# A two-sequence encoder trunk on one core: other costs on the emission clock, a scatter operand laid out by token, and attention weights as products of rounded halves

## The chip, the core and the metric

The kernel runs on one core of a Trainium2 chip as one program. The metric is the device time of one execution in microseconds (us). Three executions of the kernel before took 3652.63, 3653.04 and 3654.71 us (median 3653.04). Engines are named as in the profile: PE (TensorE; PEld is its weight load), DVE (VectorE), ACT (ScalarE), POOL (GpSimd) and SP, which here only issues transfers.

## The reference

Two sequences of 256 tokens and 1024 features go through the same two layers with the same weights.

```python
def trunk(x, p, ...):
    for i in range(DEPTH):                       # DEPTH = 2
        if i % N_MIXERS == 0:
            h = dilated_mixture_attention(x, attn_w_qkv[j], attn_w_out[j])   # layer 0
        else:
            h = short_conv_mixer(x, conv_w_in[j], conv_kernel[j], conv_w_out[j])   # layer 1
        x = layer_norm(DEEPNORM_ALPHA * x + h, ln1_gain[i], ln1_bias[i])
        f = peer_channel_mixer(x, peer_w_query[i], peer_sub_keys[i], peer_u[i], peer_v[i])
        x = layer_norm(DEEPNORM_ALPHA * x + f, ln2_gain[i], ln2_bias[i])
        x = x + jax.nn.sigmoid(x @ ple_w_gate[i]) * (p[i] @ ple_w_proj[i])
```

`dilated_mixture_attention` multiplies x (256x1024) by a matrix of 1024x9216, attends in three groups of 8 heads, and multiplies by a 1024x1024 output matrix. `peer_channel_mixer` scores each token against sub-keys, takes for each of 8 heads the 16 best of 16384 experts, and adds `gelu(x . u[e]) * gate * v[e]` over the 128 chosen experts; u and v have 16384 rows of 1024 numbers. All of it is in float32.

## The kernel before, in words

**Two threads.** `thread_a` carries the first sequence and `thread_b` the second. Each is a generator that emits instructions and yields a cost; the main loop always continues the thread with the smaller sum of costs. Thread B begins at `T0B`, thread A at 0. The sum of costs is the emission clock. It also sets the priorities by which a scheduler, at build time, writes one fixed order for each engine. On the chip each engine works through its own order. `GCOST` is the cost of four gathers, `RCOST` of one eighth of a routing, and 11, 2.5 and 22 (lines 223 to 305) those of attention.

**Experts, two ways.** Thread A gathers: for each of its two blocks of 128 tokens and each of 128 chosen experts it fetches a row of u per token (line 472, POOL issues, 128 rows of 4 KB), DVE multiplies it with x and sums (line 489), and later the same with v (line 510): 512 gathers in a layer into a ring of 8 buffers. Thread B computes densely: it reads the whole of u and v in blocks of 128 experts (`dense_u`, `down`), so 256 blocks of 512 KB in a layer, and multiplies the hidden values by a gate matrix G that is zero where an expert was not chosen. `scatter` builds G for 16 blocks at a time: DVE writes one-hot rows (line 583, tile I1) and their product with the gates, in two float16 halves (line 585, tile I0, the moving operand); PE multiplies them, one matmul for each token (line 599, 32 columns; line 592, 16 columns, for the first 16 blocks); ACT and DVE move the result out (lines 600, 601). In I0 the token is the innermost index, so the 32 columns of one token lie 64 bytes apart. While B routes, `hold` keeps A from emitting gathers.

**Attention.** `token_major_steps` (line 111) multiplies x with `w_qkv` and `w_out`: a block of 512 KB holds two slices of 128x512, and four float32 matmuls read it. There are 80 such blocks, or 320 products, in each thread's attention. `wload` brings a block into the ring `raw` (8 buffers), which also holds the norm parameters and the routing's weights while the first pools are open (`open1`). `attend` computes scores, a softmax (lines 250 to 257) and the values (line 272).

**Routing** (`route`) is a long chain of small DVE instructions (top-16 searches, lines 349 to 357, and index arithmetic to line 420). `finish` is the last gated product of a layer (`ple`).

Of the kernel before, what the change touches and what calls it, by code (L numbers as in the profile page):

```python
# [8 lines left out]
F32 = mybir.dt.float32  # L9
F8 = mybir.dt.float8e4  # L10
F16 = mybir.dt.float16
# [35 lines left out]
def encoder_trunk(ctx: ExitStack, tc: tile.TileContext, A: dict):  # L47
# [37 lines left out]
    iota16 = T(cp, [P, CH, 2 * TG], "iota16", F16)  # L85
# [10 lines left out]
    def wload(e, src, n=WB):  # L96
        raw = e.raw()[:, :n]
        nc.sync.dma_start(raw, src)
# [5 lines left out]
    def wblocks(e, name, nb, cols=512):  # L104
        kpb = WB // cols
        src = A[name]
        for b in range(src.shape[1]):
            w = wload(e, src[nb, b])
            yield b * kpb, kpb, w.rearrange("p (c n) -> p c n", n=cols)

    def token_major_steps(e, xt, name, nb, ps, kcs=KC):
        ps += [e.mm() for _ in range(NT)]
        for c0, n, w in wblocks(e, name, nb):
            for t in range(NT):
                for c in range(n):
                    kc = c0 + c
                    mm(ps[t], xt[:, kc, t * P:(t + 1) * P], w[:, c], kc == 0, kc == kcs - 1)
            yield 2.5
# [70 lines left out]
    def attention(e, g, x):  # L189
        ap = e.attn  # L190
        xt = e.xt()
        first = e.mask is None
        for kb in range(0, KC, 2):
            nc.scalar.dma_start(xt[:, kb:kb + 2].rearrange("p c s -> p (c s)"), A[f"xT{g}"][:, kb * S:(kb + 2) * S])
# [5 lines left out]
        ot = e.xt()  # L200
        done = {}

        def project(hp):
            base = (hp // 2) * 9 + (0 if hp % 2 == 0 else 5)
            qkT = T(ap, [P, NG, 4, S], "qkT", bufs=2)
            for gr in range(NG):
# [16 lines left out]
                yield 11  # L223
# [4 lines left out]
            yield 11  # L228
            if hp % 2 == 0:
                v2 = T(ap, [P, NT, 4, HD], "v2", bufs=2)  # L230
                ps = token_major(e, xt, "w_qkv", base + 4)
                for t in range(NT):
                    nc.scalar.activation(v2[:, t].rearrange("p a d -> p (a d)"), ps[t], AF.Copy)
                yield 11
            else:
                v2 = done[hp - 1][2]
            done[hp] = qkT, v01, v2

        def attend(hp):
# [20 lines left out]
            def values(hh, t, pr):  # L260
# [11 lines left out]
                nc.scalar.activation(ot[:, h, sl], ov[:, :P], AF.Copy)  # L272

            held = []
            for hh in range(2):
                for t in range(NT):
# [3 lines left out]
                    yield 2.5  # L280
# [24 lines left out]
        yield 22  # L305
# [236 lines left out]
    def peer_dense(e, i, xt, sel, spill, newx, pre):  # L542
# [30 lines left out]
        def scatter(c):  # L573
# [3 lines left out]
            for tg in range(S // TG):  # L577
                ts = slice(tg * TG, (tg + 1) * TG)
                if tg % 2 == 0:
                    t2 = slice(tg * TG, (tg + 2) * TG)  # L580
                    I1 = T(dp, [P, CH, 2 * TG], "I1", F16, bufs=1)
                    I0w = T(dp, [P, 2 * CH * 2 * TG], "I0", F16, bufs=2).rearrange("p (q a b) -> p q a b", q=2, a=CH)
# [3 lines left out]
                I0 = I0w[:, :, :, (tg % 2) * TG:(tg % 2 + 1) * TG]  # L586
                ps = T(e.phid, [P, 512], "hid").rearrange("p (a q b) -> p a q b", q=2, b=CH)
                gv = G[:, :, ts]
                if c < SCU:
                    for k in range(TG):  # L590
                        for q in range(2):
                            nc.tensor.matmul(ps[:, k, 0], J[:, tg * TG + k], I0[:, q, :, k], start=q == 0, stop=q == 1)
# [5 lines left out]
                for k in range(TG):  # L598
                    nc.tensor.matmul(ps[:, k], J[:, tg * TG + k], I0[:, :, :, k], start=True, stop=True)  # L599
# [81 lines left out]
    R1 = 8  # L681
# [14 lines left out]
    def open1():  # L696
# [4 lines left out]
        xp = p1.enter_context(tc.tile_pool(name="xt1", bufs=2))  # L701
# [3 lines left out]
        e.xt = ring(xp, [P, KC, S], "x")  # L705
# [30 lines left out]
    GCOST = 6.0  # L736
    T0B = 280.0
    RCOST = 21.0
# [96 lines left out]
def _layout(inputs):  # L835
# [46 lines left out]
    put("iota16", np.repeat(np.arange(CH, dtype=np.float16), 2 * TG)[None])  # L882
# [36 lines left out]
```

## Time and profile before

| | us |
|---|---|
| median of three runs | 3653.04 |
| profiled execution | 3650.72 |
| its span | 3648.9 |
| PE busy in the span | 3337.4 |
| DVE busy | 2191.9 |
| ACT busy | 559.7 |
| POOL busy | 1399.5 |

The profile is of one execution; the span is the time between its first and its last instruction. It was cut into ten stages by the first instructions of the norms (line 160), of the gate matrix (line 568) and of thread B's last sums (line 631): A's attention to 331.4 us, B's attention beside A's routing and first gathers to 741.7, B's routing to 917.7, the first gate matrix to 959, layer 0's dense part to 1892, `finish` and convolution of both threads with A's routing to 2330, B's routing to 2505, the gate matrix to 2545, layer 1's dense part to 3500, and the end.

### The profile page before, as it was taken

The numbers are of one execution on the slowest core, as the hardware profiler recorded it, in microseconds if no ns is written. First come the engines' busy times: TensorE is split into PE (matmuls) and PEld (weight loads), VectorE is DVE, ScalarE is ACT, GpSimd is POOL, SyncE is SP. The second block draws the span as 40 slices with busy tenths as digits, with TensorE's granted clock in tenths as the row PEclk, the third lists the DMA queues.
The fourth block names the chain that finished last, engine by engine and source line by source line (L and its number), as shares of the span: only waits on it lengthen the run. The fifth ranks groups of instructions, "written<-read, shape, count | busy, mean of one in ns | idle before, by whom it ended". The sixth has DMA issues, their size and how long they took to land. (4 is left out here: it accounts for less than half of the span.)

```text
span 3648.9 us, 42774 instructions
## 1 busy us (share of the span) xinstructions
PE 3337.4 (91%) x15472; PEld 2224.3 (61%) x15472; DVE 2191.9 (60%) x4766; ACT 559.7 (15%) x1380; POOL 1399.5 (38%) x1476
## 2 busy tenths in 40 slices
PE   9998999987699999999999859894999999999937
PEld 4555565566466666666667538583576666666623
DVE  0002796047976677766651284488866767676683
ACT  1222223223110001000011112132000001000001
POOL 0110574000355555555630040001655555555560
PEclk9999999999799999999999979896999999999978
DMA  6434797343599999999985564442999999999993
GB/s 210 136 119 127 280 347 262 110 141 116 192 377 368 374 374 368 376 374 372 391 312 169 157 222 156 141 140 75 390 366 360 369 368 360 370 375 375 406 401 113
DMA packets 280436, 1007.19 MB, mean 276 GB/s; under 512 B 31648, under 2 KB 33056, under 8 KB 280224
## 3 DMA queue, kind: packets, MB, share of 16 engines
q0 software_dynamic: 147456, 536.94, 38.7%
q1 hardware_dynamic: 124128, 448.85, 34.7%
q10 hardware_dynamic: 8640, 18.68, 1.5%
q8 instruction: 122, 2.00, 0.2%
q14 instruction: 90, 0.74, 0.1%
HBM read 999.09 MB, written 5.24 MB: 275 GB/s over the span
## 5 line engine op out<-in xcount | busy, mean ns | idle before, releaser
L472 POOL DMA_INDIRECT g<-in_u_dram,ei x512 | 635.1, 1241 | 572.8 <-DVE g L489 219.9
L102 PE MATMUL out<-ur,hs 128*128 128x512 f32 x1824 | 819.8, 600 | 35.8 <-ACT k L649 30.0
L102 PE MATMUL hid<-bx1T,ur 128*128 128x256 f32 x3584 | 817.9, 382 | 4.5 <-DVE G L601 4.5
L472 POOL DMA_INDIRECT g<-in_v_dram,ei x512 | 628.9, 1228 | 424.1 <-DVE acc L510 158.5
L102 PEld LDWEIGHTS hid<-bx1T,ur 128*128 128x128 f32 x3584 | 677.6, 191 | 137.7 <-issue 47.1
L510 DVE SCALAR_TENSOR_TENSOR acc<-g,cf,acc 128x1024 f32<-128x1024 f32 x508 | 652.1, 1284 | 56.0 <-DMA g<-in_v_dram,ei 46.4
L489 DVE SCALAR_TENSOR_TENSOR g<-g,xa 128x1024 f32<-128x1024 f32 x512 | 608.8, 1225 | 49.6 <-DMA g<-in_u_dram,ei 49.5
L102 PEld LDWEIGHTS out<-ur,hs 128*128 128x128 f32 x1824 | 339.2, 192 | 411.4 <-issue 371.1
L102 PE MATMUL mm<-raw,x 128*128 128x512 f32 x1280 | 569.9, 596 | 10.3 <-DMA x<-in_xT_dram 8.2
L102 PEld LDWEIGHTS mm<-raw,x 128*128 128x128 f32 x1280 | 237.4, 192 | 274.4 <-issue 269.2
L250 DVE SCALAR_TENSOR_TENSOR k<-tr,mask 128x512 f32<-128x512 f32 x32 | 22.0, 688 | 404.0 <-PE tr L247 404.0
L599 PEld LDWEIGHTS <-J 128*128 128x128 fp8e4 x3584 | 223.0, 112 | 62.1 <-issue 37.2
L599 PE MATMUL hid<-I,J 128*128 128x32 f16 x3584 | 245.1, 232 | 8.7 <-ACT hs L554 5.1
L102 PE MATMUL out<-bx1T,ur 128*128 128x256 f32 x1024 | 232.9, 389 | 16.9 <-ACT k L369 10.8
L102 PEld LDWEIGHTS out<-bx1T,ur 128*128 128x128 f32 x1024 | 198.5, 195 | 47.3 <-ACT k L369 13.2
L400 POOL TENSOR_TENSOR ci<-sif 128x32 f32<-128x32 f32 x64 | 17.4, 292 | 535.2 <-ACT sif L386 534.6
L600 ACT ACTIVATE G<-hid 128x256 f32<-128x256 f32 x224 | 85.9, 384 | 876.5 <-PE hid L599 876.5
L102 PE MATMUL out<-ur,x 128*128 128x512 f32 x448 | 200.6, 603 | 12.6 <-DVE x L555 12.6
L601 DVE TENSOR_TENSOR G<-G,hid 128x256 f32<-128x256 f32 x224 | 92.7, 417 | 195.2 <-ACT G L600 195.2
L214 POOL TENSOR_TENSOR rm<-k,rope 128x128 f32<-128x128 f32 x48 | 27.2, 566 | 433.4 <-ACT k L210 433.2
L555 DVE SCALAR_TENSOR_TENSOR hs<-hs,G 128x512 f32<-128x512 f32 x112 | 77.2, 689 | 178.3 <-ACT hs L554 178.3
L554 ACT ACTIVATE hs<-hid 128x512 f32<-128x512 f32 x112 | 66.9, 597 | 717.5 <-PE hid L102 484.5
(182 smaller groups left out, 2651.1 us busy)
## 6 DMA issues: line engine op xcount, KB each, us to landing
ur<-in_uT_dram SPq DMA_DIRECT2D x256, 512.0 KB, 6.9
ur<-in_v_dram SPq DMA_DIRECT2D x256, 512.0 KB, 6.7
raw<-in_w_qkv_dram SPq DMA_DIRECT2D x144, 512.0 KB, 4.3
raw<-in_w_q_dram SPq DMA_DIRECT2D x32, 512.0 KB, 4.2
ur<-in_w_q_dram SPq DMA_DIRECT2D x32, 512.0 KB, 3.6
raw<-in_c_in_dram SPq DMA_DIRECT2D x24, 512.0 KB, 3.8
ur<-in_c_in_dram SPq DMA_DIRECT2D x24, 512.0 KB, 3.6
raw<-in_w_out_dram SPq DMA_DIRECT2D x16, 512.0 KB, 4.4
```

Source lines behind the costliest of these rows:

```text
L102: nc.tensor.matmul(out, a, b, start=first, stop=last)
L214: nc.gpsimd.tensor_tensor(m1, st[:, :, :2 * RH], c, op=ALU.mult)
L250: nc.vector.scalar_tensor_tensor(prf, sc, SCALE, mask[:, t], op0=ALU.mult, op1=ALU.add)
L400: eng.tensor_tensor(dst[:, :, off:off + n], src[:, :, 1, 0:n], src[:, :, 0, a0:a0 + 1].to_broadcast([P, 2, n]), op=ALU.add)
L472: nc.gpsimd.indirect_dma_start(out=t, out_offset=None, in_=tab, in_offset=bass.IndirectOffsetOnAxis(ap=idx, axis=0))
L489: nc.vector.scalar_tensor_tensor(r, r, 1.0, x[t], op0=ALU.mult, op1=ALU.mult, accum_out=dots[:, k:k + 1])
L510: nc.vector.scalar_tensor_tensor(acc[t], r, c, acc[t], op0=ALU.mult, op1=ALU.add)
L554: nc.scalar.activation(hs, hid, AF.Gelu)
L555: nc.vector.scalar_tensor_tensor(hs, hs, 1.0 / GSC, G[:, 2 * pr:2 * pr + 2], op0=ALU.mult, op1=ALU.mult)
L599: nc.tensor.matmul(ps[:, k], J[:, tg * TG + k], I0[:, :, :, k], start=True, stop=True)
L600: nc.scalar.activation(gv, ps[:, :, 0].rearrange("p a b -> p b a"), AF.Copy)
L601: nc.vector.tensor_tensor(gv, gv, ps[:, :, 1].rearrange("p a b -> p b a"), op=ALU.add)
```

## The change

Three things are changed. First, the two matrices of attention: each block is split by ACT into a copy rounded to float32r (`hi`) and by DVE into the rounded rest (`lo`), x and the attention's output likewise, and each product becomes three matmuls, hi hi, hi lo and lo hi. The ring `raw` shrinks from 8 to 3 buffers; rings of 3 and 2 hold `hi` and `lo`. Second, in `scatter` the token becomes the outer index of I1 and I0, so the 32 columns of one token lie side by side. Third, five costs and the start of thread B on the emission clock.

```diff
+    def split(hi, lo, src):
+        nc.scalar.activation(hi, src, AF.Copy)
+        nc.vector.tensor_tensor(lo, src, hi.bitcast(F32), op=ALU.subtract)
...
+        hi, lo = e.hi()[:, :n], e.lo()[:, :n]
         nc.sync.dma_start(raw, src)
-        return raw
+        split(hi, lo, raw)
+        return hi, lo
...
     def mm(out, a, b, first, last):
-        nc.tensor.matmul(out, a, b, start=first, stop=last)
+        if not isinstance(a, tuple):
+            nc.tensor.matmul(out, a, b, start=first, stop=last)
+            return
+        nc.tensor.matmul(out, a[0], b[0], start=first, stop=False)
+        nc.tensor.matmul(out, a[0], b[1], start=False, stop=False)
+        nc.tensor.matmul(out, a[1], b[0], start=False, stop=last)
...
-                nc.scalar.activation(ot[:, h, sl], ov[:, :P], AF.Copy)
+                split(ot[0][:, h, sl], ot[1][:, h, sl], ov[:, :P])
...
-                    nc.vector.tensor_tensor(I1, iota16, ic[:, t2].unsqueeze(1).to_broadcast([P, CH, 2 * TG]), op=ALU.is_equal)
-                    bc = [P, 2, CH, 2 * TG]
-                    last = nc.vector.tensor_tensor(I0w, I1.unsqueeze(1).to_broadcast(bc), gT[:, :, t2].unsqueeze(2).to_broadcast(bc), op=ALU.mult)
+                    nc.vector.tensor_tensor(I1, iota16, ic[:, t2].unsqueeze(2).to_broadcast([P, 2 * TG, CH]), op=ALU.is_equal)
+                    bc = [P, 2 * TG, 2, CH]
+                    last = nc.vector.tensor_tensor(I0w, I1.unsqueeze(2).to_broadcast(bc), gT[:, :, t2].rearrange("p q b -> p b q").unsqueeze(3).to_broadcast(bc), op=ALU.mult)
...
-                    nc.tensor.matmul(ps[:, k], J[:, tg * TG + k], I0[:, :, :, k], start=True, stop=True)
+                    nc.tensor.matmul(ps[:, k].rearrange("p q b -> p (q b)"), J[:, tg * TG + k], I0[:, k].rearrange("p q a -> p (q a)"), start=True, stop=True)
...
-    R1 = 8
+    R1 = 3
+    H1 = 3
+    L1 = 2
...
-    GCOST = 6.0
-    T0B = 280.0
-    RCOST = 21.0
+    GCOST = 5.2
+    T0B = 420.0
+    RCOST = 14.0
+    PCOST = 17.0
```

The new costs move instructions on every engine. On DVE, in B's attention after A's routing, the order before holds only the softmax (mask and scale, maximum, reciprocal; the gathers have been stopped by then):

```order
L250 SCALAR_TENSOR_TENSOR k_749_3065<-tr_3061,mask_105 128x512
L252 TENSOR_REDUCE nm_3067<-k_749_3065 128x1
L256 RECIPROCAL rd_3071<-den_3069 128x1
L250 SCALAR_TENSOR_TENSOR k_776_3158<-tr_3154,mask_105 128x512
L252 TENSOR_REDUCE nm_3160<-k_776_3158 128x1
L256 RECIPROCAL rd_3164<-den_3162 128x1
L250 SCALAR_TENSOR_TENSOR k_819_3307<-tr_3303,mask_105 128x512
L252 TENSOR_REDUCE nm_3309<-k_819_3307 128x1
L256 RECIPROCAL rd_3313<-den_3311 128x1
```

In the order of the changed kernel the same stretch holds splits of weight blocks (line 99, `lo`), A's gathered sums (line 534, line 510 before) and the softmax, mixed:

```order
L99 TENSOR_TENSOR lo_4913<-raw_4911,hi_4912 128x1024
L534 SCALAR_TENSOR_TENSOR acc_4366<-g_5074,cf_4698,acc_4366 128x1024
L99 TENSOR_TENSOR x_2424<-tr_4691,x_2423 128x128
L99 TENSOR_TENSOR lo_4931<-raw_4929,hi_4930 128x1024
L534 SCALAR_TENSOR_TENSOR acc_4366<-g_5077,cf_4698,acc_4366 128x1024
L534 SCALAR_TENSOR_TENSOR acc_4366<-g_5080,cf_4698,acc_4366 128x1024
L99 TENSOR_TENSOR lo_4949<-raw_4947,hi_4948 128x1024
L534 SCALAR_TENSOR_TENSOR acc_4366<-g_5160,cf_4698,acc_4366 128x1024
L99 TENSOR_TENSOR lo_5088<-raw_5086,hi_5087 128x1024
L534 SCALAR_TENSOR_TENSOR acc_4366<-g_5163,cf_4698,acc_4366 128x1024
L274 SCALAR_TENSOR_TENSOR k_1096_4855<-tr_4851,mask_118 128x512
```

Each of B's splits now stands behind one or more of A's gathers. The other place is the end of layer 1. Before, DVE's order ends its work on experts with A's gathers, then both threads' norms:

```order
L510 SCALAR_TENSOR_TENSOR acc_18662<-g_21387,cf_20985,acc_18662 128x1024
L510 SCALAR_TENSOR_TENSOR acc_18662<-g_21390,cf_20985,acc_18662 128x1024
L510 SCALAR_TENSOR_TENSOR acc_18662<-g_21393,cf_20985,acc_18662 128x1024
L514 SCALAR_TENSOR_TENSOR xa_6_99<-xa_6_99,acc_18662 128x1024
L160 BN_STATS lnst_21398<-xa_6_99 128x6
L160 BN_STATS lnst_21855<-G_21833 128x6 x2
```

In the changed kernel it ends with B's dense part alone (line 579 multiplies hidden values by G, line 625 adds to G):

```order
L625 TENSOR_TENSOR G_22919<-G_22919,hid_23491 128x16x16
L579 SCALAR_TENSOR_TENSOR hs_23567<-hs_23567,G_22919 128x512
L579 SCALAR_TENSOR_TENSOR hs_23603<-hs_23603,G_22919 128x512
L579 SCALAR_TENSOR_TENSOR hs_23639<-hs_23639,G_22919 128x512
L579 SCALAR_TENSOR_TENSOR hs_23675<-hs_23675,G_22919 128x512
L579 SCALAR_TENSOR_TENSOR hs_23711<-hs_23711,G_22919 128x512
```

A's last gather now stands 30 pairs of blocks ahead of B's last.

## Rows read from the trace of the kernel before

**Rows 1.** Busy time of the ten stages: the four engines, PE clock, DMA, GB/s.

```profile
0.00:331.40 331.40, 318.58 (x995) 164.09 (x996) 25.16 (x49) 70.51 (x139) 34.40 (x100) 0.99 0.45 148
331.40:741.70 410.30, 393.13 (x1362) 226.39 (x1361) 237.16 (x743) 109.01 (x269) 168.23 (x236) 0.98 0.65 235
741.70:917.70 176.00, 136.60 (x624) 115.68 (x622) 117.23 (x564) 53.20 (x143) 10.24 (x56) 0.89 0.41 135
917.70:959.00 41.30, 16.30 (x520) 15.47 (x520) 37.78 (x62) 7.05 (x20) 5.57 (x4) 0.50 0.09 27
959.00:1892.00 933.00, 927.60 (x4586) 630.07 (x4587) 667.69 (x952) 88.12 (x200) 536.41 (x425) 0.99 0.98 374
1892.00:2330.00 438.00, 373.13 (x1450) 270.99 (x1449) 193.73 (x708) 74.82 (x222) 46.83 (x116) 0.92 0.52 169
2330.00:2505.00 175.00, 140.87 (x630) 116.57 (x628) 118.05 (x572) 52.90 (x143) 10.31 (x56) 0.89 0.41 130
2505.00:2545.00 40.00, 14.26 (x512) 14.16 (x512) 36.52 (x56) 7.89 (x19) 6.87 (x4) 0.50 0.11 32
2545.00:3500.00 955.00, 941.84 (x4616) 635.89 (x4616) 675.19 (x968) 82.44 (x192) 539.30 (x443) 0.99 0.98 374
3500.00:3648.90 148.90, 75.09 (x184) 34.97 (x184) 83.35 (x99) 13.80 (x33) 41.31 (x39) 0.76 0.60 223
```

**Rows 2.** Waits of DVE in layer 0's dense stage: us in total, times, longest.

```profile
DVE G L601 <- ACT G L600: 96.4, 38, 4.4
DVE hs L555 <- ACT hs L554: 84.8, 28, 5.4
DVE I L585 <- PE hid L599: 48.8, 46, 3.5
```

**Rows 3.** Matmuls by line and form: busy us, mean ns; idle before.

```profile
L102 PE MATMUL mm<-raw,x 128*128 128x512 f32 x1280 | 569.9, 596 | 10.3 <-DMA x<-in_xT_dram 8.2 <-ACT x L272 1.5 <-ACT v L227 0.5
L592 PE MATMUL hid<-I,J 128*128 128x16 f16 x1024 | 28.5, 188 | 39.7 <-DVE I L585 39.7
L102 PE MATMUL av<-x,raw 128*128 128x256 f32 x640 | 143.0, 385 | 15.0 <-ACT k L369 14.7 <-ACT x L145 0.2
L102 PE MATMUL av<-raw,x 128*128 128x512 f32 x192 | 83.9, 592 | 1.6 <-DMA x<-hd 1.6
```

**Rows 4.** PE in the dense stage, in order of time: start, us, count.

```profile
1500.29 1.07 PE L599 MATMUL hid<-I,J 128*128 128x32 f16 x16
1501.18 3.67 PE L102 MATMUL out<-ur,hs 128*128 128x512 f32 x8
```

**Rows 5.** ACT and DVE instructions by line and form: busy us, mean ns; idle before.

```profile
L222 ACT ACTIVATE qkT<-tr 128x512 f32<-128x512 f32 x48 | 26.8, 595 | 81.8 <-PE tr L221 81.6
L583 DVE TENSOR_TENSOR I<-iota,ic 128x512 f16<-128x512 f16 x128 | 54.0, 422 | 0.5
L585 DVE TENSOR_TENSOR I<-I,gT 128x1024 f16<-128x1024 f16 x128 | 89.1, 696 | 96.4 <-PE hid L599 89.1 <-PE hid L592 6.3
L568 DVE TENSOR_TENSOR I<-iotaj,jT 128x1024 f16<-128x1024 f16 x16 | 18.9, 1221 | 0.1
```

**Rows 6.** DVE at the start of the dense stage, gathers back to back.

```profile
950.97 1.28 DVE L510 SCALAR_TENSOR_TENSOR acc<-g,cf,acc 128x1024 f32<-128x1024 f32 x1
952.16 1.22 DVE L489 SCALAR_TENSOR_TENSOR g<-g,xa 128x1024 f32<-128x1024 f32 x1
...
953.31 1.22 DVE L489 SCALAR_TENSOR_TENSOR g<-g,xa 128x1024 f32<-128x1024 f32 x1
```

**Rows 7.** The last 32 gathers on DVE, with nothing beside them.

```profile
3521.30 42.23 DVE L510 SCALAR_TENSOR_TENSOR acc<-g,cf,acc 128x1024 f32<-128x1024 f32 x32
```

**Rows 8.** The gathers' queue (packets, MB, share), and issues (KB each, us to landing).

```profile
q0 software_dynamic: 147456, 536.94, 38.7%
...
raw<-in_w_qkv_dram SPq DMA_DIRECT2D x144, 512.0 KB, 4.3
```

More of the change, by code (lines that the diff above doesn't have):

```diff
@@ L94, in encoder_trunk, with wload, at, wblocks @@
         pass
-    def wload(e, src, n=WB):
+    def split(hi, lo, src):
+        nc.scalar.activation(hi, src, AF.Copy)
+        nc.vector.tensor_tensor(lo, src, hi.bitcast(F32), op=ALU.subtract)
+    def wload(e, src, n=WB, parts=False):
         raw = e.raw()[:, :n]
+        if not parts:
+            nc.sync.dma_start(raw, src)
+            return raw
+        hi, lo = e.hi()[:, :n], e.lo()[:, :n]
         nc.sync.dma_start(raw, src)
-        return raw
-    def mm(out, a, b, first, last):
-        nc.tensor.matmul(out, a, b, start=first, stop=last)
-    def wblocks(e, name, nb, cols=512):
+        split(hi, lo, raw)
+        return hi, lo
+    def at(ops, *ix):
+        if isinstance(ops, tuple):
+            return tuple(o[(slice(None),) + ix] for o in ops)
+        return ops[(slice(None),) + ix]
+    def mm(out, a, b, first, last):
+        if not isinstance(a, tuple):
[4 more added lines that the diff above has]
+        nc.tensor.matmul(out, a[1], b[0], start=False, stop=last)
+    def wblocks(e, name, nb, cols=512, parts=False):
         kpb = WB // cols
@@ L107, in wblocks @@
         for b in range(src.shape[1]):
-            w = wload(e, src[nb, b])
-            yield b * kpb, kpb, w.rearrange("p (c n) -> p c n", n=cols)
+            w = wload(e, src[nb, b], parts=parts)
+            cut = lambda z: z.rearrange("p (c n) -> p c n", n=cols)
+            yield b * kpb, kpb, tuple(map(cut, w)) if parts else cut(w)
     def token_major_steps(e, xt, name, nb, ps, kcs=KC):
         ps += [e.mm() for _ in range(NT)]
-        for c0, n, w in wblocks(e, name, nb):
+        for c0, n, w in wblocks(e, name, nb, parts=isinstance(xt, tuple)):
             for t in range(NT):
@@ L190, in attention @@
         ap = e.attn
-        xt = e.xt()
+        xt = e.xs(), e.xs()
         first = e.mask is None
         for kb in range(0, KC, 2):
-            nc.scalar.dma_start(xt[:, kb:kb + 2].rearrange("p c s -> p (c s)"), A[f"xT{g}"][:, kb * S:(kb + 2) * S])
+            hi, lo = (z[:, kb:kb + 2].rearrange("p c s -> p (c s)") for z in xt)
+            raw = e.raw()[:, :2 * S]
+            nc.scalar.dma_start(raw, A[f"xT{g}"][:, kb * S:(kb + 2) * S])
+            split(hi, lo, raw)
         if first:
@@ L591, in scatter @@
                         for q in range(2):
-                            nc.tensor.matmul(ps[:, k, 0], J[:, tg * TG + k], I0[:, q, :, k], start=q == 0, stop=q == 1)
+                            nc.tensor.matmul(ps[:, k, 0], J[:, tg * TG + k], I0[:, k, q], start=q == 0, stop=q == 1)
                     nc.scalar.activation(gv, ps[:, :, 0].rearrange("p a b -> p b a"), AF.Copy)
@@ L704, in open1 @@
         e.raw = e.ln = ring(w, [P, WB], "raw")
-        e.xt = ring(xp, [P, KC, S], "x")
+        e.hi = ring(w, [P, WB], "hi", F32R, H1)
+        e.lo = ring(w, [P, WB], "lo", F32R, L1)
+        e.xs = ring(xp, [P, KC, S], "x", F32R)
         e.mm, e.tr, e.sc = ring(pm, [P, 512], "mm"), psring(ptr, "tr"), psring(ptr, "tr")
@@ L881, in _layout @@
     put("ident", np.eye(P, dtype=np.float32))
[L882 removed]
+    put("iota16", np.tile(np.arange(CH, dtype=np.float16), 2 * TG)[None])
     put("iotaj", np.arange(NK // 4, dtype=np.float16)[None])
```

25 lines of the change are left out of this document (13 added, 12 removed).

## The prediction

> **What bounds the kernel now.** I read the busy time by stage first, because PE's share over the whole span (91%) mixes stages with different limits. In [rows 1] the reader is to see three kinds. In both attention stages (331.4 and 410.3 us) and both dense stages (933 and 955 us) PE is busy 96 to 99% of the time: it is the bound. In B's two routings (176 and 175 us) and the two gate matrices (41 and 40 us) PE waits for chains of small DVE instructions; DVE is busy 117 us of 176, and the other 59 are gaps within the chain. The last 148.9 us are A's remaining gathers, then both threads' `finish`. Second, DVE's waits: in the dense stage DVE is busy 667.7 us of 933 and waits 230 for PE and for evictions of PE's results [rows 1, 2]; it has that much to spare. Third, the DMA: its engines are busy 98% there at 374 GB/s [rows 1], yet PE never waits for a block, so it is full but not yet late.
>
> From the order of DVE I counted where A's 512 gathers of each layer stand, before and after the change. Layer 0: during B's attention 76, then 183; during B's routing 0, then 57; dense stage 436, then 272. Layer 1: in the dense stage of layer 0 and during B's `finish` and convolution 20, then 113 and 160; during B's routing 0, then 23; dense stage 492, then 216. So A runs ahead of B: its `finish`, convolution and routing of layer 1 come to lie inside B's dense stage of layer 0, and the end is B's alone. The time is summed below along B's stages.
>
> **Attention products.** A float32 product of 128x512 takes two instructions; 1280 of them were busy 569.9 us [rows 3], so 0.445 us each and 0.890 a product. At the granted clock of 1.00 (2.4 GHz) 0.445 us are 1068 cycles for 512 columns, two per column and instruction, four per product: both halves of one operand with both of the other. No row shows a product of operands that are already rounded. Its bounds: one of the four parts, 0.2226 us, or one whole instruction as shown, 0.445. I take 0.2226, since a rounded operand has no second half to pass. Three then cost 0.668 us and an attention of 320 products saves 71 us of PE. The Trainium skill (FP8 and Floating Point Precision, TensorE Precision Notes) gives true float32 four passes and a reduced form that truncates what it reads. By it three products are three quarters of one, the same 71 us; no run here shows it.
>
> **Splits.** 160 blocks of 128x1024 need one ACT copy and one DVE subtraction each. ACT's 128x512 takes 0.595 us [rows 5], so at most 1.19 a block: 95 us beside 70.5 busy of 331.4 in A's attention; PE covers it. On DVE the nearest row of 1024 float32 from two tensors is the gather's product, 1.15 us from start to start [rows 6]: 92 us an attention. In A's attention DVE is busy 25 us, so this is hidden. If ACT and DVE gave no cover, a block would cost 2.3 us, 187 us an attention. The ring of three: a landing takes 4.3 us [rows 8], the two halves of the split 2.3, so three blocks every 6.6 us, against 2.67 us of products each: enough. Stage A: 331.4 - 71 + 12 (first split ahead of the first product 4, uneven starts 8, an estimate) = 272 us.
>
> **B's attention becomes DVE's.** In the new order DVE has between A's and B's first norm 80 splits (92 us), 103 and 80 gathered sums at 1.15 and 1.20 us [rows 6] (118 and 96), a routing with its norm (117) and 16 softmaxes (25, as in A's attention) [rows 1]: 448 us. The same sum for the order before, with 76 gathers, is 231 where DVE was busy 237.2 [rows 1]. PE would need 393 - 71 = 322. So DVE sets this stage, and a faster product buys nothing here. I add 42 us for gaps: the routing's chain has 59 by itself, which gathers and splits partly fill, and the norm's parameters take two of three `raw` buffers. Stage B: 490 us, bounds 455 and 530 (before 410.3). Queued behind each late split are B's products, the routing's products behind these on PE, and gathers on POOL.
>
> **B's routing.** 117 us of DVE and 57 gathers (25 x 1.15 + 32 x 1.20 = 67 us) and 3 splits make 188; a third of the gathers fill gaps that exist anyway. 195 us, bounds 185 and 215 (before 176). Layer 1: 118 + 27 stay under 175; 177.
>
> **Scatter.** 16 matmuls of 32 columns run from 1500.29 to 1501.18 us, 55.6 ns each [rows 4], at a granted clock of 0.99 (2.4 GHz) [rows 1]. Those of 16 columns take 28.5/1024 = 27.8 ns [rows 3] in stages with a granted clock of 0.50 (1.2 GHz) [rows 1]. 1.74 ns a column at both clocks: the reading of the operand sets it, not the array. Side by side I expect the 27.8 that a pair of weight load and matmul has been seen to need; the bounds are 55.6 and 13.3 (32 columns at 2.4 GHz). 56 pairs of blocks a layer with 32 matmuls each: 1792 x 27.8 ns = 50 us of PE a layer. The Trainium skill (SBUF — State Buffer, Specifications) says that SBUF is read in lines of 16 bytes and that each change of line costs unless it is hit twice; steps of 64 bytes change it at every column. By that rule the step is the cause and the 50 us are there; by the rows alone a fixed price per column would fit too, and they are not (a rival below). On DVE the one-hot rows lose speed: a broadcast along the innermost index takes 1221 ns for 1024 float16, the present form 696 [rows 5]; line 583 by the same slope 422 to about 690. 128 x (525 + 268) ns = 101 us, 50 a layer, inside the 230 that DVE waits. Without that cover it would cost the full 101.
>
> **Dense stages.** Layer 0: 933 - 50 = 883, plus A's work that now lies there: 143.0 us of 256 columns, two thirds of 83.9, and some 10 of transposes and the like (an estimate) [rows 3] = 209, plus 24 for waits between A's chain and PE's order: 1116 us. DMA: 237 gathers of 0.524 MB (536.94/1024) [rows 8] lie beside 39 of 64 pairs; with their 140 blocks that is 198 MB in 883 x 39/64 = 538 us, 368 GB/s, where 374 at 98% are seen [rows 1]. It just fits; I add nothing and keep 1090 and 1150 as bounds. Layer 1: 955 - 50 + 28 (A's third of the 83.9) = 933. The gate matrices: 46 and 45, as 8 gathers and the slower one-hot rows stand ahead of the first product.
>
> **Between the layers.** B's `finish` and convolution now run with 160 gathers: 83.9 MB and 44 blocks, 107 MB. At 374 GB/s 286 us; at the pace of the last gathers, 42.23/32 = 1.32 us [rows 7] or 397 GB/s, 269. I take 278 (before 438, with both threads in it).
>
> **The end.** A's gathers end 30 pairs before B. B's sums, norm and `finish` alone: half of PE's 75 us [rows 1] and 17 for sums and norm: 55 (before 148.9).
>
> **Sum.** 272 + 490 + 195 + 46 + 1116 + 278 + 177 + 45 + 933 + 55 = 3607, with 1.8 us outside the span 3609. The profiled execution was 2.3 us under the median, so the forecast is 3611 us, 1.2% below it. Terms against before: -59, +80, +19, +5, +183, -160, +2, +5, -22, -94. Much of the change is exchange: what leaves the end is paid in B's attention.
>
> **Rivals.** (1) Slower: a rounded product costs more than a quarter. At 0.445 us A's attention grows by 213 us and B's, with 322 + 213 = 535 of PE plus gaps, by about 69: 3893. It decides from 0.267 us on, where A's 960 products eat the 42 us of gain. For it: each instruction shown needs two cycles a column; against it: two such instructions already make all four parts. (2) Slower: the step of 64 bytes is not what the scatter pays; 100 us come back: 3711. For it the equal price per column; against it that a twofold clock leaves it unchanged. (3) Slower: DVE, serving splits, gathers and softmax in one order, stalls on each in turn; B's attention, routing and the stretch between the layers come out at their upper bounds and a little more: 3690. (4) No change: the terms meet at 3650, with B's attention at 520. (5) Faster: the gaps are filled wholly and DMA gives 397 GB/s: B's attention 455, between the layers 250, no stalls in the dense stage: 3514.
>
> **How the numbers follow.** Forecast 0.44 (own range 3545 to 3645); (5) 0.15; (4) 0.10; (3) 0.11; (2) 0.08; (1) 0.12. Faster by over 0.2% is forecast and (5), 0.59; within 0.2%, about what this measurement can tell from no change, is (4), 0.10; slower is the rest, 0.31. The range 3490 to 3740 leaves out (1) and the far edges.
>
> **What would show it.** A's first norm near 272 us and the new products at 0.22 us show the first term; above 0.27 the forecast fails. B's first norm near 762 with DVE over 90% busy shows the second. Scatter groups of 16 in 0.45 us instead of 0.89 show the third; PE waiting there for blocks would mean that DMA took its place. A's layer-1 routing inside B's first dense stage and an end of 55 us show the rest.

## The result and the profile after

The changed kernel takes 3739.53 us (median of 4 runs) against 3652.84 of the kernel before on the same chip: a ratio of 1.0238, 95% interval 1.022 to 1.0256. It is slower by 2.4% where I had forecast 3611 us, faster by 1.2%; the time lies at the upper edge of the range. The table shows the same ten stages as [rows 1], cut at the same events, within 2 us but for one (the end of the first dense part, see below): each stage's span and length, then busy us of PE, PE's weight loads, DVE, ACT and POOL with the number of instructions, PE's granted clock, the DMA's share and GB/s.

```profile
0.00:277.80 277.80, 258.29 (x1298) 216.52 (x1299) 127.72 (x145) 152.73 (x222) 51.43 (x100) 1.00 0.51 167
277.80:822.90 545.10, 385.26 (x1693) 308.83 (x1692) 459.64 (x1009) 200.03 (x364) 325.72 (x341) 0.86 0.79 279
822.90:1041.40 218.50, 139.48 (x636) 119.63 (x635) 190.69 (x663) 50.35 (x142) 81.91 (x115) 0.81 0.70 260
1041.40:1083.00 41.60, 15.53 (x515) 14.40 (x513) 40.70 (x50) 8.30 (x21) 4.01 (x3) 0.50 0.05 14
1083.00:2247.40 1164.40, 1114.42 (x5504) 752.42 (x5504) 783.65 (x1494) 149.98 (x372) 517.46 (x453) 0.98 0.83 310
2247.40:2531.50 284.10, 152.08 (x560) 105.12 (x560) 229.11 (x309) 30.50 (x68) 185.28 (x176) 0.77 1.00 383
2531.50:2719.40 187.90, 129.46 (x608) 112.67 (x608) 153.16 (x628) 55.03 (x152) 42.77 (x82) 0.83 0.54 187
2719.40:2761.00 41.60, 23.55 (x557) 18.50 (x558) 40.51 (x48) 6.90 (x18) 9.93 (x3) 0.53 0.10 27
2761.00:3688.20 927.20, 913.01 (x4648) 595.46 (x4647) 440.20 (x609) 89.70 (x195) 272.41 (x205) 1.00 0.70 259
3688.20:3739.70 51.50, 41.08 (x103) 19.01 (x101) 15.77 (x23) 9.20 (x20) 0.00 (x0) 0.92 0.33 112
```

Stage by stage, measured and (in brackets) forecast, in us: A's attention 278 (272), B's attention 545 (490), B's routing 218.5 (195), gate matrix and first dense stage 1206 (1162), between the layers 284 (278), routing 188 (177), gate matrix and second dense stage 969 (978), end 51.5 (55). Three stages carry 122 of the 133 us by which the spans differ: B's attention 55, the dense stage with its gate matrix 44, B's routing 23. In B's attention no engine is busy for more than 460 of 545 us; PE's granted clock is 0.86 there (0.98 before).

Who waits for whom in B's attention: us in total, times, the longest.

```profile
PE mm L118 <- ACT k L393: 72.0, 3, 36.0
PE tr L245 <- POOL k L242: 38.2, 18, 7.8
PE mm L121 <- DVE lo L99: 29.0, 21, 5.4
PE mm L120 <- ACT hi L98: 8.9, 6, 4.4
...
DVE lo L99 <- ACT hi L98: 33.8, 9, 21.4
DVE g L513 <- DMA g<-in_u_dram,ei: 17.5, 9, 4.8
DVE k L274 <- PE tr L271: 15.0, 3, 6.1
...
ACT qkT L246 <- PE tr L245: 56.4, 18, 7.4
ACT hi L98 <- DMA raw<-in_w_qkv_dram: 48.6, 22, 7.4
```

The reader is to see two things. The engines wait in a ring: PE for POOL (the rotary product, line 242), for DVE (the rest `lo`) and for ACT (the rounded half `hi`); DVE for ACT, for gathered rows and for PE; ACT for PE and for blocks of weights. And the longest sum stands outside that ring: three waits of PE, 72 us of its 160 idle, are for ACT's copy in A's routing (line 393). In B's attention of the kernel before, PE waited 2.8 us for POOL and at most 6.8 for any other.

The products and the one-hot rows, by line and form: busy us and mean ns of one; idle time before.

```profile
L121 PE MATMUL mm<-lo,x 128*128 128x512 f32 x640 | 267.7, 418 | 31.7 <-DVE lo L99 31.7
...
L122 PE MATMUL mm<-hi,x 128*128 128x512 f32 x640 | 259.1, 405 | 0.5 <-DVE x L99 0.5
L120 PE MATMUL mm<-hi,x 128*128 128x512 f32 x640 | 243.7, 412 | 26.0 <-ACT hi L98 25.6 <-ACT x L98 0.4
L99 DVE TENSOR_TENSOR lo<-raw,hi 128x1024 fp32r<-128x1024 f32 x160 | 199.4, 1247 | 137.1 <-PE mm L121 73.0 <-ACT hi L98 38.7 <-ACT k L234 12.8
...
L609 DVE TENSOR_TENSOR I<-I,gT 128x1024 f16<-128x1024 f16 x128 | 156.4, 1222 | 92.9 <-PE hid L623 91.4
...
L623 PE MATMUL hid<-I,J 128*128 128x32 f16 x3584 | 124.6, 177 | 25.4 <-DVE G L625 11.5 <-ACT hs L578 11.5 <-DVE I L609 2.4
```

In A's attention the products follow each other at an even pace; these are the first and the last of ten, in order of time (start, us):

```profile
119.42 0.39 PE L122 MATMUL mm<-hi,x 128*128 128x512 f32 x1
...
121.46 0.39 PE L120 MATMUL mm<-hi,x 128*128 128x512 f32 x1
```

(121.46 - 119.42) / 9 = 0.227 us from start to start: the quarter that I took (0.2226). The scatter's busy time halves (245.1 to 124.6 us), and the one-hot rows cost what [rows 5] foretold (1222 ns). The unit prices stood; the sum over a stage did not.

### The profile page after: what moved, and what is told of

It is laid out like the page before. It is cut to its first block, busy times and chain, and to the rows that moved or that the text cites. A ratio compares the mean times of both kernels' runs of the same rounds, so it can differ in the third digit from the quotient of the medians.

```text
span 3739.7 us, 44761 instructions
## 1 busy us (share of the span) xinstructions
PE 3172.2 (85%) x16112; PEld 2262.6 (61%) x16112; DVE 2481.2 (66%) x4966; ACT 752.7 (20%) x1573; POOL 1490.9 (40%) x1476
## 5 line engine op out<-in xcount | busy, mean ns | idle before, releaser
L496 POOL DMA_INDIRECT g<-in_u_dram,ei x512 | 664.6, 1298 | 498.6 <-DVE acc L534 164.8
L496 POOL DMA_INDIRECT g<-in_v_dram,ei x512 | 643.8, 1258 | 364.2 <-DVE acc L534 107.2
L513 DVE SCALAR_TENSOR_TENSOR g<-g,xa 128x1024 f32<-128x1024 f32 x512 | 611.8, 1222 | 57.2 <-DMA g<-in_u_dram,ei 56.4
L121 PE MATMUL mm<-lo,x 128*128 128x512 f32 x640 | 267.7, 418 | 31.7 <-DVE lo L99 31.7
L99 DVE TENSOR_TENSOR lo<-raw,hi 128x1024 fp32r<-128x1024 f32 x160 | 199.4, 1247 | 137.1 <-PE mm L121 73.0
L118 PE MATMUL out<-bx1T,ur 128*128 128x256 f32 x1024 | 234.6, 391 | 50.3 <-ACT k L393 36.8
L120 PE MATMUL mm<-hi,x 128*128 128x512 f32 x640 | 243.7, 412 | 26.0 <-ACT hi L98 25.6
L122 PE MATMUL mm<-hi,x 128*128 128x512 f32 x640 | 259.1, 405 | 0.5 <-DVE x L99 0.5
L609 DVE TENSOR_TENSOR I<-I,gT 128x1024 f16<-128x1024 f16 x128 | 156.4, 1222 | 92.9 <-PE hid L623 91.4
L98 ACT ACTIVATE hi<-raw 128x1024 fp32r<-128x1024 f32 x160 | 168.4, 1057 | 133.8 <-PE mm L122 65.9
L121 PEld LDWEIGHTS mm<-lo,x 128*128 128x128 f32 x640 | 126.0, 197 | 67.1 <-DVE lo L99 42.8
L623 PEld LDWEIGHTS <-J 128*128 128x128 fp8e4 x3584 | 120.3, 96 | 76.1 <-issue 53.0
```

The costliest lines, as they stand in the source:

```text
L98: nc.scalar.activation(hi, src, AF.Copy)
L99: nc.vector.tensor_tensor(lo, src, hi.bitcast(F32), op=ALU.subtract)
L120: nc.tensor.matmul(out, a[0], b[0], start=first, stop=False)
L121: nc.tensor.matmul(out, a[0], b[1], start=False, stop=False)
L122: nc.tensor.matmul(out, a[1], b[0], start=False, stop=last)
L496: nc.gpsimd.indirect_dma_start(out=t, out_offset=None, in_=tab, in_offset=bass.IndirectOffsetOnAxis(ap=idx, axis=0))
```

## The experiments

All are compared with the kernel before, run beside them; lengths of stages are from their profiles. "Clock of before" means the emission numbers of before (gather 6.0, B's start 280, routing 21, projections 11, attention 2.5 and 22), "the new clock" those of the change; PE's granted clock is always called so. Code is cut to the lines that matter, some joined into one.

**The parts one by one.** First everything but the clock, then the clock alone, then the scatter and the products alone.

```
-    GCOST, T0B, RCOST, PCOST = 5.2, 420.0, 14.0, 17.0   # and yields 5.0, 35
+    GCOST, T0B, RCOST, PCOST = 6.0, 280.0, 21.0, 11.0   # and yields 2.5, 22
```

The second is the same edit the other way round, in the kernel before. The third, in the kernel before:

```
-  I0w = ... .rearrange("p (q a b) -> p q a b", q=2, a=CH)    # I1, iota16 and I0 alike
+  I0w = ... .rearrange("p (b q a) -> p b q a", q=2, a=CH)
```

The fourth is the first with this edit undone.

> The changed kernel with the emission clock of before (gather 6, thread B starts at 280, routing 21, projections 11, attention steps 2.5 and 22); products of rounded halves and the scatter layout stay. Theory 'clock': the loss is 107 more gathers in B's attention and 57 in its routing, which DVE serves in one order with 80 splits. In this order B's attention holds 76 gathers and DVE has 327 us of work there instead of 448, so PE is the bound again: B's attention near 360 us (545 in the changed kernel), its routing near 176 (218). The gathers that go back to the dense stages meet a DMA that is 98% busy there, so the scatter's 100 us are only half seen. In all 3460 to 3540 us. Rival 'splits': the new products cost the loss by themselves (ACT, then DVE, and a ring of three blocks): B's attention stays over 480 and the time over 3650.

> The kernel before with the new emission clock alone: float32 products, old scatter. Theory 'clock': 169 gathers come to stand in B's attention and 71 in its routing, and no splits; PE needs 393 us there and DVE 339, so B's attention grows a little (430 to 480), the routing by 30, the dense stages gain a few us of DMA only, and the end is B's alone; 3650 to 3760 us, that is same or slower. Rival 'the clock is good for the order, the splits are what it cannot bear': the exchange without splits pays, 3550 to 3630.

> The kernel before with the scatter operand laid out by token, nothing else. Theory 'access step': the 32-column matmuls fall from 55.6 ns to about 35 as in the changed kernel's trace, 37 us a layer of PE; DVE's one-hot rows grow by 50 us a layer under cover. If PE is the bound in the dense stages: 3570 to 3590 us. Rival 'DMA': the dense stages hold 436 and 492 gathers, the DMA is 98% busy at 374 GB/s, and what PE gains is lost to waits for blocks or to a later end: 3630 to 3660. Rival 'one-hot rows': DVE's 100 us more delay G: over 3660.

> The kernel before with the products of rounded halves and the ring of three alone; clock and scatter of before. Theory 'clock': both attentions get shorter, A's by 54 us (331 to 278), B's by 50 (410 to 360), and nothing else moves: 3540 to 3570 us. Rival 'splits': DVE's 92 us of subtractions and the ring of three eat it in B's attention, where 76 gathers stand too: B's attention 400 or more, time 3600 or more. Rival 'given back': A reaches its gathers 54 us earlier but B's dense stage is bound by the DMA, so a third of the gain comes back at the end: 3580.

Measured: products and scatter without the new clock 3563.1 us, ratio 0.9735 (0.9719 to 0.9751), faster, with B's attention at 442.6, between the two answers; the new clock alone 3802.33, 1.0392 (1.0375 to 1.041), slower as its theory had it, and above what either theory gave; the scatter alone 3577.73, 0.9778 (0.9761 to 0.9794), the first theory; the products alone 3637.11, 0.9945 (0.9927 to 0.9963), the rival. So the new clock costs 143 us without the other two parts and 177 with them (by the spans of the profiles), and turns a gain into a loss; the scatter keeps 73 us of its 100 by the profiles (81 by the medians); and the products, worth 54 us in A's attention, lose 32 in B's (442.7 against 410.3) with the same 76 gathers there. B's attention with the clock of before and both other parts, the same columns as above:

```profile
278.10:720.70 442.60, 366.58 (x1682) 298.62 (x1681) 334.54 (x842) 189.78 (x353) 191.93 (x236) 0.92 0.64 221
```

and in the kernel with the new clock alone (float32 products, 169 gathers), with its gate matrix and first dense stage below:

```profile
327.20:790.60 463.40, 404.53 (x1369) 232.79 (x1368) 346.90 (x888) 117.99 (x279) 299.18 (x328) 0.94 0.84 310
...
1027.40:2245.50 1218.10, 1172.23 (x6019) 812.65 (x6017) 757.62 (x1528) 158.95 (x391) 489.92 (x440) 0.97 0.80 290
```

In the first row neither PE (367) nor DVE (335) comes near 443: my theory that DVE alone paces the stage needed a test. The kernel with the scatter alone shows where its 100 us went. In gate matrix and first dense stage PE is 905.4 us busy where it was 953.6 before, so 48 of the 50 are there, but the stage is only 36.7 shorter (984.0 to 947.3): PE idles 42 us where it idled 30, with the DMA at 0.96. The stretch before, then with the scatter alone:

```profile
919.20:1903.20 984.00, 953.60 (x5132) 649.73 (x5131) 704.70 (x1004) 95.76 (x221) 541.98 (x428) 0.97 0.95 358
918.20:1865.50 947.30, 905.42 (x5131) 597.93 (x5129) 753.23 (x1005) 90.86 (x219) 543.86 (x428) 0.97 0.96 371
```

**DVE's rest, the norm's parameters, B in float32.** The first leaves the rest of B's weights out: the rounded half stands in its place. The first two are edits of the changed kernel, the third of the one with the clock of before; there B's blocks also get the eight buffers of all three rings:

```
         raw = e.raw()[:, :n]
+        if in_thread_b:
+            nc.scalar.activation(hi, raw, AF.Copy)
+            return hi, hi
         split(hi, lo, raw)
```

```
-        gb = ln_params(e, which, i)
+        if e is env[1]:
+            z = newbx().rearrange("p c s -> p (c s)")
+            gb = z[:, :D], z[:, D:]          # and two DMAs into them
```

```
-        xt = e.xs(), e.xs()
+        xt = (e.xs(), e.xs()) if first else e.xs().bitcast(F32)   # ot alike
```

> The changed kernel, but thread B's weight blocks are not split: the rounded half stands for the rest too, so 80 subtractions of 1.24 us leave DVE in B's attention and its second products use the wrong part (the rest of B's weights is left out); ACT's copies, the 960 products and the new clock stay. The order then holds 168 gathers in B's attention and 72 in its routing. Theory 'one order on DVE': with 347 us of DVE instead of 449, B's attention falls from 545 to 440 to 470, near the 463 of the float32 kernel with the same clock; its routing is 15 us longer for 15 more gathers; the whole 3650 to 3680. Rival 'products and DMA': the 85 us of gaps come from PE's products at the lower granted clock and from blocks that land late; B's attention stays over 510 and the time over 3700.

> The changed kernel with the first norm's parameters of both threads in a buffer of their own (that of the transposed x, free at that time) instead of two of the three raw buffers of the weights. Theory 'ring of three': the wait of 21 us at the start of B's attention, where DVE waits for ACT's copy and this for the blocks, goes, and with it 20 to 30 us of the 545; the whole 3705 to 3720. Theory 'one order on DVE': gathers are what DVE is behind with, the 21 us come back in front of the next split; 3730 to 3745.

> The clock of before and the new scatter layout; products of rounded halves in thread A's attention alone, float32 products in B's, with B's blocks in the eight buffers of the three rings in turn. Theory 'the split pays only where DVE is idle': A's attention 278, B's 405 to 415 instead of 443 and PE-bound again, dense stages as in the kernel with the clock of before: 3520 to 3540 us, the fastest so far. Rival 'B's attention of 443 is due to A's gathers starting earlier, not to the splits': B's attention over 430 and no gain over 3563.

Measured: without the rest 3701.25, 1.0099 (1.0082 to 1.0116), B's attention 471.3; with the norm's parameters apart 3746.96, 1.0221 (1.0203 to 1.0239); with float32 in B 3550.07, 0.9684 (0.9667 to 0.9701). Without DVE's 104 us of subtractions (and with 15 of the gathers moved on to the routing) B's attention is 74 us shorter under the new clock, just above the first theory's range; 32 of the 74 are PE's waits for A's routing, 39.6 us there where the change has 72.0. The whole is slower than the theory said, since the routing (240) and the stretch from the first dense stage to the second gate matrix (483) got 22 and 18 us longer. The norm's parameters do not matter: B's attention stays at 547.6, and the 21 us wait is still there, so the theory of the ring's two lost buffers falls. The kernel with float32 in B is faster than the 3563.1 with all splits: A's attention 279, B's 415 and bound by PE again:

```profile
279.20:694.20 415.00, 395.01 (x1379) 230.13 (x1378) 240.70 (x746) 111.61 (x270) 163.15 (x236) 0.98 0.65 236
```

Its time is 10 us over my bound: the two dense stages with their gate matrices, where the DMA stands at 0.95 and 0.96, gave back 25 us of the 28 won in B's attention.

**The rest left out under the clock of before, and the lengths alone.** The first joins two edits shown; the second, in the changed kernel:

```
-    GCOST, RCOST = 5.2, 14.0
+    GCOST, RCOST = 6.0, 21.0
```

> The changed kernel with the clock of before (B's attention 443 us there, PE busy 367 of it, DVE 335), and again without the split's rest in thread B (the rounded half stands for the rest, 80 subtractions of 1.24 us leave DVE; ACT's copies and the 960 products stay). Theory 'one order on DVE': with 240 us of DVE work PE is the bound; the granted clock stays near 1.0 and B's attention comes to 335 to 365 us, which is what the quarter-price products promised; a part is given back in the dense stages, whose gathers are the same: 3470 to 3510. Rival 'PE': the products themselves take 367 at the lower granted clock, or ACT's copies pace them: B's attention 410 or more, the time over 3530.

> The changed kernel with the costs of a pair of gathers (6.0) and of a routing step (21) as before; the attention's lengths (17, 5, 35 and the start of B at 420) stay as changed. By the order 154 gathers stand in B's attention (183 in the change, 76 with the old clock), 18 in its routing (57, 0), and A's routing of layer 1 leaves B's routing. Theory 'every gather that leaves the dense stage for B's attention costs there': B's attention 510 to 525, its routing 185 to 195; A's layer-1 work still lies in B's first dense stage: 3660 to 3720 us. Rival 'the lengths are harmless, the gathers' and the routing's costs do it': within 30 us of the 3563 with the whole clock of before.

Measured: without the rest 3528.27, 0.9652 (0.9635 to 0.9668), B's attention 423.7 and not 335 to 365; with the lengths alone 3649.41, 0.999 (0.998 to 1.0), B's attention 500.3 with 154 gathers, its routing 194.1, whole and attention a little under the theory's ranges and far from the rival (A's layer-1 work did not move into the first dense stage, where I had put it). The first is a miss for my theory: the stage falls to the rival's side, the time just under the rival's 3530. With 246 us of DVE work the stage is only 19 us shorter. B's attention there, and what PE waits for:

```profile
278.80:702.50 423.70, 357.06 (x1687) 297.61 (x1686) 245.78 (x765) 189.90 (x353) 163.98 (x236) 0.92 0.66 232
```

```profile
PE tr L250 <- POOL k L247: 34.3, 9, 6.8
PE mm L125 <- ACT hi L111: 18.3, 8, 7.0
PE tr L165 <- DVE xa L201: 7.6, 1, 7.6
```

PE now waits for POOL, whose rotary products stand between the issues of A's gathers and small sums of A's routing, and for ACT and its blocks.

**Gathers or products.** B's rotary products on DVE, without and with the split's rest; and all splits, but no gather in B's attention, each with the clock of before:

```
-                    nc.gpsimd.tensor_tensor(m1, ...)        # and the three after it
+                    rp = nc.gpsimd if first else nc.vector
+                    rp.tensor_tensor(m1, ...)
```

```
             pri[0] = PG
+            if i == 0:
+                yield 400.0
```

> The kernel with the clock of before and without the split's rest in thread B (B's attention 424 us, PE idle 67 of it), with B's rotary products moved from POOL to DVE (96 instructions, some 30 us of DVE). Theory 'POOL's queue': PE's 34 us of waits for POOL go, the clock stays higher, B's attention 375 to 395, the time 3490 to 3505. Rival 'gathers and DMA': PE then waits for ACT's copies and their blocks; B's attention over 410, the time within 10 us of 3527.

> The changed kernel with the clock of before, splits whole, with B's rotary products on DVE. PE waits 23 us for POOL and 31 for DVE's rest in B's attention of 443. Theory 'POOL's queue' would have it 425 or less, the time near 3545. Theory 'one order on DVE': the products for the rotation queue behind the same gathers and splits there, B's attention 440 to 465, the time 3560 to 3585.

> The changed kernel with the clock of before and all splits, but A's gathers of layer 0 begin 400 later on the clock: none of the 512 stands in B's attention (76 otherwise), 444 in the first dense stage. DVE has 237 us in B's attention. Theory 'gathers': without them on POOL, DMA and DVE the rounded products are worth what was forecast, B's attention 335 to 360 instead of 443, PE over 93% busy; the dense stages get 40 MB more for a DMA that is full, and lose 60 to 110 of it again: 3540 to 3620 in all. Rival 'products': splits and lower granted clock alone hold B's attention over 400, and the time is 3600 to 3680.

Measured: rotary products on DVE without the rest 3518.34, 0.9602 (0.9586 to 0.9618), B's attention 406.8, between the two answers, the time the rival's; the same with the rest 3563.63, 0.9728 (0.9712 to 0.9744), B's attention 447.8, as one order on DVE has it; and without gathers in B's attention 3640.83, 0.9942 (0.9925 to 0.9958), B's attention 386.9, between again, the time the rival's. POOL's queue is worth 17 us where DVE has no rest to subtract and nothing where it has: PE then waits 51.7 us for DVE instead. The 76 gathers are worth 56 us of this stage. B's attention without them:

```profile
277.30:664.20 386.90, 347.00 (x1683) 286.06 (x1683) 246.14 (x717) 181.80 (x344) 83.64 (x160) 0.97 0.45 150
```

and PE's waits with rotary products on DVE and all splits:

```profile
PE mm L121 <- DVE lo L99: 51.7, 22, 7.4
PE mm L120 <- ACT hi L98: 10.1, 6, 5.0
```

The gathers pushed out came back in other places: against the same kernel with its gathers in place, the stretch from the first dense stage to the second gate matrix is 98 us longer and the end 29.

**The scatter's step.** Three layouts in the kernel before, with the columns of one matmul 4, 8 and 16 bytes apart.

```
-  I0w ... .rearrange("p (b q a) -> p b q a", q=2, a=CH)      # layout by token: 2 bytes
+  I0w ... .rearrange("p (b a q) -> p b q a", q=2, a=CH)      # 4 bytes
+  I0w ... .rearrange("p (g q a b) -> p g q a b", b=4)        # 8 bytes; b=8: 16 bytes
```

> The kernel before with the scatter operand laid out by token, but the two parts interleaved, so that a column is 4 bytes from the next where the layout by token alone has 2 and the kernel before 64. Rule 'lines of 16 bytes' (the Trainium skill, SBUF — State Buffer, Specifications): four columns share a line, a 32-column matmul stays near 35 to 40 ns, and the time is near the 3578 of the layout alone. Rival 'any step over 2 bytes': 55 ns as before, dense stages 940 to 985 long, 3640 to 3665 us. DVE's second one-hot row writes with a step of 4 bytes then and may take longer than 1222 ns; its own row tells this apart.

> The kernel before with the scatter operand in groups of 4 tokens, so that the columns of one matmul stand 8 bytes apart (64 before); DVE's second one-hot row is written in 8 pieces. Read only the 32-column matmuls: by lines of 16 bytes, with two columns to a line, about 35 ns (176 in the row, which counts to the modelled end); by a price for any step over 4 bytes, 55 ns, as before.

> The same in groups of 8 tokens, columns 16 bytes apart, the second one-hot row in 4 pieces. By lines of 16 bytes each column is in a new line: 55 ns as with 64 bytes. By a limit elsewhere (32 or 64 bytes): 35 ns.

Measured: 4 bytes 3593.14, 0.9809 (0.9793 to 0.9825); one run each of 8 bytes, 3580.64, and 16 bytes, 3664.2 (before 3654.26). The scatter's row with 2 bytes, then 8, then 16 (with 4 bytes 125.7 us); that of 64 bytes was 245.1:

```profile
L599 PE MATMUL hid<-I,J 128*128 128x32 f16 x3584 | 125.5, 176 | 17.1 <-DVE G L601 13.7 <-ACT hs L554 2.8 <-issue 0.6
```

```profile
L601 PE MATMUL hid<-I,J 128*128 128x32 f16 x3584 | 158.1, 196 | 12.1 <-DVE G L603 8.5 <-ACT hs L554 3.5
```

```profile
L601 PE MATMUL hid<-I,J 128*128 128x32 f16 x3584 | 253.0, 237 | 4.0 <-DVE G L603 2.8 <-ACT hs L554 1.3
```

2 and 4 bytes cost the same, 8 bytes a little more; the large step is between 8 and 16 bytes, not at the first step that leaves adjacency, and 16 bytes cost about what 64 did. In order of time the layout by token runs 16 of them in 0.40 us, 25 ns each against 55.6 [rows 4]:

```profile
1504.02 0.55 PE L599 MATMUL hid<-I,J 128*128 128x32 f16 x16
1504.42 7.11 PE L102 MATMUL out<-ur,hs 128*128 128x512 f32 x16
```

The Trainium skill (SBUF — State Buffer, Specifications) has lines of 16 bytes that want at least two hits each for full bandwidth; with 8 bytes there are two, with 16 one. The trace agrees on the large step (253.0 us at 16 bytes); the rise from 125.7 to 158.1 at 8 bytes, where two hits remain, it does not explain.

## Why the prediction was wrong

**What held.** The price of a rounded product (0.227 against 0.2226 us), A's attention (278 against 272; PE is 60 us less busy there, where I had 71), the subtraction (1247 ns against some 1150), the one-hot rows, the step as the scatter's cause, the 160 gathers between the layers (284 against 278), the end (51.5 against 55). Rivals (1) and (2) are out. DVE's own sums held too: 460 us busy in B's attention against 448 foretold, 191 in the routing against 188. One reason was luck: I took the equal price per column of the scatter's 16 and 32 columns as a sign that reading the operand sets both, but with the layout by token the 32 columns fell to 25 ns and the 16 did not fall at all (28.5 us busy before, 30.0 with the scatter alone). And rival (5) was added up wrongly: its terms make some 3523, and 397 GB/s gives 269 us between the layers, not 250; nothing hangs on it.

**The step that failed: "B's attention becomes DVE's ... Stage B: 490".** I took PE's sum (322) and DVE's (448), let the greater set the stage, and added 42 us of gaps. DVE's sum came out; its gaps were 85 us. And the stage is no maximum of two sums, as the runs with the clock of before show. With all splits and no gathers it lasts 387, though PE's work is 347 and DVE's 246; with 76 gathers, and no other cost changed, 443. That is 56/76 = 0.73 us a gather, though no engine was full. As I read the waits, each gather lengthens the chain from block over ACT and DVE to PE, and that from ACT over POOL to PE's transposes; a product that is a quarter shorter leaves PE less work to wait behind.

With 154 gathers the stage lasts 500 (the lengths alone), with 183 545 (the change). These steps, 0.74 and 1.5 us a gather, are no price of a gather, for the costs changed with them and another wait came in. PE idles 160 us in the change against 76 with the clock of before, and 72 of the 84 us between them are three waits for A's routing. What ACT waits for in the change; then this wait of PE with the lengths alone, and the only one behind line 393 with the clock of before:

```profile
ACT k L393 <- DVE ef L444: 36.9, 4, 19.0
...
PE mm L118 <- ACT k L393: 31.3, 3, 17.0
...
PE tr L399 <- ACT k L393: 1.4, 1, 1.4
```

Line 118 here multiplies A's tokens with the routing's weights; it needs a buffer that ACT's copy (line 393) frees, and ACT stands behind DVE's index arithmetic (line 444), among gathers and splits. While PE waits there, B's products stand behind it in PE's order. The same stretch of time in the change, then with the clock of before:

```profile
364.00:520.00 156.00, 80.70 (x329) 65.40 (x329) 139.68 (x399) 36.09 (x82) 99.47 (x103) 0.74 0.83 294
...
364.00:520.00 156.00, 110.74 (x444) 86.53 (x443) 138.65 (x346) 51.66 (x89) 116.14 (x109) 0.85 0.85 309
```

DVE works equally long in both, and PE gets 30 us less done. So of the 58 us from 443 to 500 this wait is 31, and of the 45 from 500 to 545 it is 41. Float32 products under the new clock take 53 us for 93 more gathers, with 36.8 us of the same wait.

So the term of 490 was 55 short: 12 in DVE's sum and 43 in its gaps. The 71 us that the products were to save on PE in B's attention were a loss of 32 already without the new clock. PE's own 322 was short as well: it is busy 347 us without gathers, 367 with 76 and 385 in the change, at granted clocks of 0.97, 0.92 and 0.86, lower the longer PE idled (40, 76 and 160 us).

**Routing: "a third of the gathers fill gaps".** That much did, but my sum did not follow the sentence. With the clock of before the routing takes 178.7 with no gather, in the change 218.5 with 57: it grew by 40 us and DVE's busy time by 69, so 29 went into gaps. I had 71 us of DVE's work to add (188 less 117); two thirds of that on 176 make 223. My 195 left only 7 us of gaps beside DVE's 188, where 28 remained.

**First dense stage, 44 short with its gate matrix.** 11 us are a slip of mine: I cut the stage at 1892, but PE goes on with B's dense products, and B's last sums (line 631) begin at 1903.2. The two rows of these products at and behind that cut in the kernel before:

```profile
1891.19 7.03 PE L102 MATMUL out<-ur,hs 128*128 128x512 f32 x16
...
1898.71 6.60 PE L102 MATMUL out<-ur,hs 128*128 128x512 f32 x15
```

A's layer-1 work on PE is 219 us there (1172.2 of the new clock alone less 953.6) and not 209; the scatter saves 48 and not 50; PE's idle time is 50 where 29 were in the sum; the gate matrix is 4 shorter. The remaining 5 of PE's work I have no cause for.

**The sign.** Against the kernel with the clock of before, the clock's exchange gives 106 us at the end and 133 from the first dense stage's end to the second gate matrix, and takes 102 in B's attention, 40 in its routing, 257 in the first gate matrix and dense stage and 17 in the second: a loss of 177. The 219 us of A's PE work had lain where PE was idle for 98 of 599 us, and moved to a stage where PE was full; gathers went from beside PE-bound products to stages that they lengthen. I had written that much of this is exchange, and never summed the clock alone; its price was inside the stages' sums, where the mistakes of B's attention and routing hid. Rival (3), DVE stalling on splits, gathers and softmax in one order, came nearest at 3690: B's attention and its routing did come out over their upper bounds (545 over 530, 218.5 over 215), the stretch between the layers close to its own (284 against 286). It holds in part: leaving the rest out is worth 74 us under the new clock and 19 under the old, and the first dense stage was not in it.

**Open.** How the 56 us of 76 gathers divide between POOL's issue, the DMA and DVE was not settled: leaving out DVE's rest and moving POOL's rotary products brings the 443 to 407, but neither was tried without gathers, so what of these 36 us the gathers own is not known. The ring of three buffers was not tried by itself: float32 in B got eight, so what of the 28 us is the ring's and what the split's is not known. Which of the new costs puts A's routing in PE's way was not separated, and but for the lengths alone and the late gathers no other set of numbers on the clock was tried.

## What to carry to other kernels

A stage whose work passes from one engine to the next for every block is not the longest engine's sum: price it by runs of the same chain at two loads that differ in nothing else, and name the wait that grew before you call the slope a price. Work that was hidden has a place as well as a size; before moving it, sum the change of order by itself, with every other edit left out. And make a product faster only where the engines that feed it are idle: in A's attention the same split gave 54 us; in B's, with its smaller ring, it cost 28 against float32.

## What the runs showed of the hardware

POOL's rotary products slow down beside DVE's subtractions: in A's attention, with no gather near, POOL is busy 51.4 us for the same 100 instructions that took 34.4 before ([rows 1] and the first row after). The 96 of 128x64 have a median of 318 ns and a mean of 614 in the change (318 and 351 before); in A's attention the longest took 1306 (327 before), most of a subtraction more. The Trainium skill (SBUF — State Buffer, SBUF: two separate sides) says that a DVE operation with two inputs in SBUF and a GpSimd operation that reads SBUF lock each other out for a whole instruction. The trace agrees: two of these products take 1.58 us where a subtraction runs beside them, and two others 0.59 us after it (start, us; the subtraction, 1.23 us elsewhere, takes 1.46 here):

```profile
101.44 1.58 POOL L241 TENSOR_TENSOR rm<-k,rope 128x64 f32<-128x64 f32 x2
...
103.40 0.59 POOL L241 TENSOR_TENSOR rm<-k,rope 128x64 f32<-128x64 f32 x2
...
101.10 1.46 DVE L99 TENSOR_TENSOR lo<-raw,hi 128x1024 fp32r<-128x1024 f32 x1 [1.89 <-ACT k L234]
```

A rounded-float32 matmul of 128x512 starts every 0.227 us at a granted clock of 1.00 (2.4 GHz), 1.06 cycles a column. And the scatter's 32-column matmul, with its weight load, needs 25 ns from start to start where its columns lie side by side (granted clock 1.00), less than the 27.8 that I took from the 16-column one.
